# Moving the weight split and the rotary tables between engines at the start of a two-layer decoder trunk

## The chip, the cores and the metric

The kernel runs on one core of one Trainium2 chip. The metric is the device time of one execution in microseconds (us). Three executions of the kernel before gave 498.42, 498.47 and 500.37 us; their median is 498.47 us. One more execution was recorded by the hardware profiler, and every row shown below comes from that one.

A core has five engines that matter here, each with its own queue that is worked strictly in order: TensorE for matrix products (PE in the profile; its weight loads are PEld), VectorE (DVE), ScalarE (ACT), GpSimd (POOL) and SyncE (SP), which here only starts transfers (DMA).

## The reference

Two layers (`DEPTH = 2`) over 512 tokens of width 1024. A layer normalizes the stream, multiplies it with one wide matrix, splits the product into four groups of heads, mixes each in its own way, gates them, and adds the output projection to the stream:

```
h = rmsnorm(x, norm_g)
p = h @ w_in                                   # 1024 -> 3488 columns
(cq, ckv, kr, g_a, c_h, c_b, c_c, g_b, sg_u, sg_v, g_c, mq, mk, mv, g_d) = split(p)
q  = rmsnorm(cq)  @ mla_w_uq                   # latent attention, rotary part by rope(...)
kv = rmsnorm(ckv) @ mla_w_ukv
o_a = causal attention(q, k, v)
o_b = c_b * short_conv(c_c * c_h, conv_w)
o_c = spatial_gate(sg_u, sg_v, ...)
o_d = moba_attention(mq, mk, mv)               # rotary on a quarter of each head
y = concat(o_a*silu(g_a), o_b*silu(g_b), o_c*silu(g_c), o_d*silu(g_d))
x = x + y @ w_out
```

`rope(x, pos)` turns pairs of columns by the angle `pos * 500000^(-2i/32)`. So a table of 16 cosines and 16 sines for each of the 512 tokens is needed: two tiles of 128 partitions x 4 x 16.

## The kernel before, in words

**Precision.** TensorE multiplies in a shortened float format. So each operand is split in two: a high half (the value rounded to that format) and a low half (the value minus the high half), and each product is three matmuls: high x high, low weight x high, high weight x low. For a weight tile the names are `raw_` (as loaded), `whi_` and `wlo_`; for the stream they are `hTh` and `hTl`. The q projection of latent attention uses `whi_uq`, the kv projection `whi_ukv`, the next projection `raw_sq` (split into `yTh` and `yTl`, which serve as its weight tiles).

**The first stage** (`c_first`, inside `main`) computes `cq`: the first 416 columns of layer 0. It runs over the 8 slices k of 128 rows of the weight. For each k, TensorE transposes the slice of x (`xT`, four transposes), ACT rounds it to `hTh` (`x_parts`), DVE makes `hTl`, and then come 4 matmuls (one per group of 128 tokens) with `whi·hTh`, 4 with `wlo·hTh`, 4 with `whi·hTl`. The slices 6 and 7 come in another order: token group by token group, so that the first group is finished early. ACT also squares x for the normalization (`junk`, accumulated in `xsum`, in `x_stats`). The four weight tiles `c0` to `c3` are each split in two halves by `split_units`: the high half on DVE (a copy), the low half by `low_half`, on GpSimd for nearly all of them (`LOVEC = 1`).

**The rotary tables** (`rope_tables`) are worked out on DVE between that work: the angle is brought into a small range in three steps, halved, and the sine and cosine of the half are summed as polynomials, one after the other, in tiles of 128 x 64 (`rope_scratch`, results `sinT` and `cosT`).

**What sets the order.** Nothing here is ordered by hand. While the kernel is written out, a planner (`Order`, `Chain`) keeps an estimated clock for each engine (`o.clk["V"]`, `["A"]`, `["G"]`) and lets many small generators take turns; each call of `ch.dve`, `ch.act`, `ch.pool` or `ch.pe` writes one instruction and moves a clock on. Several choices are made by these clocks: which engine splits a later weight tile (line 419), which one applies the rotation (`on_dve`, line 763), and which one squares for a norm (`head_sums`, line 777). So an edit in the first 30 us changes the order, and some of the engines, of instructions much later. The instruction streams that result are fixed: on the chip an engine waits for its next instruction, however late that is.

**Loads.** `load_units` issues the weight loads on SyncE's queue in a fixed order. A tile of weights can be loaded when its `raw` buffer is free, and the queue runs only a limited number of transfers ahead: the profile shows an issue waiting for the landing of an earlier transfer.

**Later stages.** After `cq` come q and kv (`low_chain`), the big projections (`sq`, `kv`, `ga` and so on), both attentions, the mixer and the output projection (`seven`), and the same for layer 1. `rms` factors are made on GpSimd as a power (`pow_rstd`; rows `xv`, `ms`, `mq`, `mk`, `mmq` on POOL). `krt` is the shared rotary key; `t0a` are the first transposes of latent attention.

Of the kernel before, what the change touches and what calls it, by code (L numbers as in the profile page):

```python
# [33 lines left out]
AHEAD = 4  # L34
NWARM, FILL, FILLEND = 6, 0.9, 15000.0
MIXT, MIXLAG, ROWT, GT = 42000.0, 2000.0, 27000.0, 27000.0
KSPLIT, SQPOOL, LOVEC = 6, 700.0, 1
PAIRS = {}
LOPRIO = -5
ROPEB, ROPES = 400.0, 900.0  # L40
EARLY = ('sq0', 'sq1', 'sq2')
YORDER, YCUT = (2, 3, 0, 1, 4, 6, 5, 7), 6
WORDER = (1, 0, 2, 3)
# [14 lines left out]
def split_const(v, bits):  # L58

    e = math.floor(math.log2(abs(v))) + 1  # L60
    q = 2.0 ** (e - bits)
    a = round(v / q) * q
    return a, v - a
# [78 lines left out]


LAT, PELAT, SLACK, PEMARGIN = 130.0, 220.0, 300.0, 80.0


def free_size(ap):
# [56 lines left out]
def cost(n):  # L204
    return max(n / 2.4, 107.0) + 2.0
# [3 lines left out]
def hybrid_trunk(ctx: ExitStack, tc: tile.TileContext, x, positions, norm_g, w_c, w_f, w_t, w_o, mla_q_norm_g,  # L209
# [3 lines left out]
    V, A, G, PE = nc.vector, nc.scalar, nc.gpsimd, nc.tensor  # L213
# [16 lines left out]
    o = Order()  # L230
# [171 lines left out]
    def split_units(i0, i1):  # L402
        for u in order[i0:i1]:
            ch = Chain(o)
            if u.name != "c0_0":
                yield from ch.wait(u.loaded)
            u.hi, u.lo = yield from u.slots.get(ch, u.name)
            n = u.a * u.b
            for i in range(2):
                if u.name == "c0_0":  # L410
                    yield from ch.wait(u.landed[i])
                while ch.t > o.now + SLACK:
                    yield ch.t - SLACK
                while not u.wanted and max(o.clk["A"], o.clk["V"]) > o.now + WSLACK:
                    yield o.now + 100.0
                sl = slice(i * n // 2, (i + 1) * n // 2)
                c2 = Chain(o, max(o.now, ch.t))
                hi, lo, raw = u.hi[:, sl], u.lo[:, sl], u.raw[:, sl]
                if o.clk["V"] + 600.0 < o.clk["A"] or u.idx < 4:
                    yield from c2.dve_fast(V.tensor_copy, hi, raw)  # L420
                else:
                    yield from c2.act(A.activation, hi, raw, AF.Copy)
                if u.idx < 4:
                    o.set(u.high[i], c2.t)
                    o.spawn(low_half(u, i, c2, lo, raw, hi), None, LOPRIO)
                    continue
                yield from c2.dve(V.tensor_tensor, lo, raw, hi.bitcast(F32), op=ALU.subtract)
            if u.idx < 4:
                continue
            ch.t = c2.t  # L430
            u.raw_slots.put(ch)
            o.set(u.ready, ch.t)

    def low_half(u, i, ch, lo, raw, hi):
        if i == 0 or u.idx < LOVEC or o.clk["V"] + 300.0 > o.clk["G"]:
            yield from ch.pool(G.tensor_tensor, lo, raw, hi.bitcast(F32), op=ALU.subtract)
        else:
            yield from ch.dve(V.tensor_tensor, lo, raw, hi.bitcast(F32), op=ALU.subtract)
        o.set(u.half[i], ch.t)
        if u.half[1 - i].t is not None:  # L440
            ch.t = max(ch.t, u.half[1 - i].t)
            u.raw_slots.put(ch)
            o.set(u.ready, ch.t)
# [42 lines left out]
    G.tensor_copy(junk[0:NT, P:2 * P], junk[0:NT, 0:P].bitcast(I32))  # L486
    for i in range(16):
        G.memset(inv[:, i:i + 1], THETA ** (-i * 2.0 / 32))
    rope_ev = Event()

    def rope_tables():
        ch = Chain(o)
        sc = yield from t2S.get(ch, "rope_scratch")
        def carve(i):
            return sc[:, i * 64:(i + 1) * 64].rearrange("p (t i) -> p t i", t=NT)

        ang, z, cp, sp = (carve(i) for i in range(4))
        kk = [carve(4 + i) for i in range(3)]

        ch.slack = ROPES  # L500

        def on_vector():
            while max(o.clk["V"], ch.t) > o.now + ROPES:
                yield max(o.clk["V"], ch.t) - ROPES

        def dv(f, *a, **k):
            yield from on_vector()
            yield from ch.dve(getattr(V, f), *a, **k)

        def stt(out, in0, c, in1, op0, op1):  # L510
            yield from on_vector()
            yield from ch.dve(V.scalar_tensor_tensor, out, in0=in0, scalar=c, in1=in1, op0=op0, op1=op1)

        for t in range(NT):
            yield from dv("tensor_scalar", ang[:, t, :], inv, posf[:, t:t + 1], None, op0=ALU.mult)
        magic = 12582912.0
        r1, r2 = [], []
        for k, m in zip(kk, (2.0 ** 22, 2.0 ** 11, 1.0)):
            c = TWO_PI * m
            ca, cr = split_const(c, 13)  # L520
            cb, cc = split_const(cr, 13)
            yield from dv("tensor_scalar", k, ang, 1.0 / c, magic, op0=ALU.mult, op1=ALU.add)
            yield from dv("tensor_scalar", k, k, magic, None, op0=ALU.subtract)
            yield from stt(ang, k, -ca, ang, ALU.mult, ALU.add)
            r1.append((k, cb))
            r2.append((k, cc))
        for k, c in r1 + r2:
            yield from stt(ang, k, -c, ang, ALU.mult, ALU.add)
        yield from dv("tensor_scalar", ang, ang, 0.5, None, op0=ALU.mult)
        yield from dv("tensor_tensor", z, ang, ang, op=ALU.mult)  # L530
        yield from dv("tensor_scalar", sp, z, -1.0 / math.factorial(15), None, op0=ALU.mult)
        yield from dv("tensor_scalar", cp, z, 1.0 / math.factorial(16), None, op0=ALU.mult)
        for n in (14, 12, 10, 8, 6, 4, 2):
            yield from stt(cp, cp, (-1.0) ** (n // 2) / math.factorial(n), z, ALU.add, ALU.mult)
            if n > 2:
                yield from stt(sp, sp, (-1.0) ** ((n - 1) // 2) / math.factorial(n - 1), z, ALU.add, ALU.mult)
        yield from dv("tensor_scalar", cp, cp, 1.0, None, op0=ALU.add)
        yield from stt(sp, sp, 1.0, ang, ALU.add, ALU.mult)
        yield from stt(sinT, sp, 2.0, cp, ALU.mult, ALU.mult)
        yield from dv("tensor_tensor", z, sp, sp, op=ALU.mult)  # L540
        yield from dv("tensor_scalar", cosT, z, -2.0, 1.0, op0=ALU.mult, op1=ALU.add)
        t2S.put(ch)
        o.set(rope_ev, ch.t)

    def bcast(src, offset, n, name):
# [86 lines left out]
    xsum = cst.tile([P, NT, KT // 2], F32, name="xsum")  # L632
    xv = cst.tile([P, 5, NT], F32, name="xv")
    v_ev, r_ev, rh_ev = Event(), Event(), Event()
    one_box, rh_box, rh_put = [], [], shared(hS, 14)
    RV, RR, RE, RE64, REE = range(5)

    def rv(i, t):
# [53 lines left out]
    def x_row():  # L692

        ch = Chain(o)
        yield from ch.wait(r_ev)
        d = yield from t2S.get(ch, "rd")
        yield from ch.pool(G.tensor_tensor, d.rearrange("p (t c) -> p t c", t=NT),
                           ident.unsqueeze(1).to_broadcast([P, NT, P]),
                           xv[:, RR, :].unsqueeze(2).to_broadcast([P, NT, P]), op=ALU.mult)
        tp = yield from trS.get(ch, "rrow")  # L700
        yield from ch.pe(4 * cost(S), PE.matmul, tp, one_box[0][:, 0:P].bitcast(F32), d, start=True, stop=True)
        zzS.put(ch)
        t2S.put(ch)
        rh_box.append((yield from hS.get(ch, "rh")))
        yield from ch.act(A.activation, rh_box[0][:, 0:S], tp, AF.Copy, scale=0.5)
        trS.put(ch)
        o.set(rh_ev, ch.t)
# [1032 lines left out]
    def start():  # L1740
        o.clk["D"] = 1000.0
        cw = Chain(o)
# [1 line left out]
            xk[kp] = yield from v4S.get(cw, f"x{kp}_0", [P, NT, 2 * P], F32)  # L1744
        load_xk(0, 1)
        wp = yield from sS.get(cw, "warm")
        one_box.append((yield from zzS.get(cw, "ones", F32R)))
        ones = one_box[0][:, 0:P].bitcast(F32)
        V.memset(ones, 1.0)
        A.activation(xsum[:, 0, 0:1], ones[:, 0:1], AF.Square, scale=D ** -0.5)  # L1750
# [2 lines left out]
            o.fill()  # L1753
        PE.transpose(wp[:, 256:256 + NT + KT], junk[0:NT + KT, P:2 * P], ident[0:NT + KT, 0:NT + KT])
        V.tensor_copy(pg, wp[:, 256:256 + NT + KT])
        o.pe_end, o.fill_until = 3300.0, FILLEND
        o.clk["V"] = 3700.0

        def fill_end():
# [73 lines left out]
```

## Time and profile before

| what | value |
|---|---|
| median of three executions | 498.47 us |
| the profiled execution's own time | 498.7 us |
| its span, first to last instruction | 497.0 us |
| PE busy | 486.4 us (98%) |
| DVE busy | 401.6 us (81%) |
| ACT busy | 311.7 us (63%) |
| POOL busy | 158.1 us (32%) |
| data moved by DMA | 81.98 MB |

The profiled execution took 1.7 us more than its span, which lies around it. A timeline row reads: start in us, duration in us, engine, line, operation, output<-inputs, shape, count, and in brackets how long the engine had been idle and what ended that. Line 166 and line 196 are the planner's helpers through which nearly all instructions are written, so rows are told apart by their tiles. Row groups (`x8 | 8.7, 1107`) give the count, the sum in us and the mean in ns. Rows of waits give: who waited, for whom, us in total, times, longest. A row of the windows view gives the stretch, then the busy us (and number of instructions) of each engine, the granted TensorE clock (1.00 is full), the DMA share and GB/s.

### The profile page before, as it was taken

To read this page: it belongs to the slowest core of one execution; us is meant where nothing else is said; L and a number is where in the kernel's file an instruction comes from. 1 tells how busy PE (TensorE), PEld (TensorE's weight loads), DVE (VectorE), ACT (ScalarE), POOL (GpSimd) and SP (SyncE) were. 2 spreads that over 40 slices of the span, in tenths; PEclk is the share of its full clock that TensorE was granted. 3 is DMA by queue.
4 is the path that set the end of the run, shared out by engine and by line. 5 is a ranking of instruction groups with operands and counts; after the bars stand their busy time and mean duration, and the time that the engine had idled before them with its cause. 6 is when DMAs were issued, how large, how long until landed. Compare 5 with 4: busy or idle time off the path is not lost.

```text
span 497.0 us, 7795 instructions
## 1 busy us (share of the span) xinstructions
PE 486.4 (98%) x2457; PEld 412.8 (83%) x2457; DVE 401.6 (81%) x1046; ACT 311.7 (63%) x899; POOL 158.1 (32%) x276
## 2 busy tenths in 40 slices
PE   8889999999999999999999999999999999999996
PEld 8677887888888888888889988888888888888886
DVE  6979986677989878689799789577888889665982
ACT  5579754587786784346566895575757676524640
POOL 4437996544132013100042478435441010000000
PEclk9999999999999999999999999999999999999999
DMA  8635539535377126876573242557449465475652
GB/s 282 196 104 178 171 106 225 190 69 102 118 219 185 51 71 192 296 274 212 166 260 128 85 117 97 211 129 141 93 134 251 167 171 105 167 261 188 226 175 85
DMA packets 37393, 81.98 MB, mean 165 GB/s; under 512 B 7132, under 2 KB 19432, under 8 KB 37096
## 3 DMA queue, kind: packets, MB, share of 16 engines
q1 hardware_dynamic: 28880, 73.09, 43.9%
q0 software_dynamic: 8448, 8.39, 11.3%
q8 instruction: 19, 0.31, 0.3%
q14 instruction: 22, 0.18, 0.1%
q10 hardware_dynamic: 24, 0.01, 0.0%
HBM read 73.61 MB, written 24.64 MB: 198 GB/s over the span
## 4 chain that ended last, share of the span: by engine, by line
PE 83%; DMA 5%; POOL 4%; ACT 3%; DVE 2%; issue 1%; SPq 1%; POOLq 0%
PE kv L196 8%; PE oy L196 6%; PE sq L196 5%; PE ch L196 4%; PE cc L196 4%; PE gd L196 4%; PE cb L196 4%; PE gb L196 4%; PE su L196 4%; PE gc L196 4%; PE ox L196 4%; PE oz L196 4%; PE sa L196 3%; PE cq L196 3%; PE ga L196 2%; PE oa L196 2%
## 5 line engine op out<-in xcount | busy, mean ns | idle before, releaser
L166 ACT ACTIVATE pd<-pd,mnd 128x256 f32<-128x256 f32 (+3 forms) x52 | 28.0, 550 | 2.6 <-DVE mnd L166 2.5
L166 ACT ACTIVATE pa<-pa,mna 128x256 f32<-128x256 f32 (+3 forms) x45 | 24.5, 558 | 5.5 <-DVE mna L166 5.5
L166 ACT ACTIVATE pha<-pTa 128x512 fp32r<-128x512 f32 (+3 forms) x32 | 13.8, 436 | 21.1 <-PE pTa L196 21.0
L196 PE MATMUL kv<-whi_kv,hTh 128*128 128x512 f32 x64 | 26.6, 416 | 0.0
L166 POOL TENSOR_TENSOR chs<-chs,rh 128x512 f32<-128x512 f32 x6 | 9.3, 1545 | 51.7 <-ACT chs L166 37.2
L196 PE MATMUL kv<-whi_kv,hTl 128*128 128x512 f32 x64 | 25.1, 392 | 0.0
L196 PE MATMUL kv<-wlo_kv,hTh 128*128 128x512 f32 x64 | 25.0, 391 | 0.0
L341 POOL DMA_DIRECT2D t<-in_w_o_dram x16 | 18.0, 1147 | 21.5 <-DMA t<-t 13.5
L166 DVE TENSOR_TENSOR pla<-pTa,pha 128x512 fp32r<-128x512 f32 (+3 forms) x32 | 15.3, 485 | 11.7 <-ACT pha L166 11.6
L166 ACT ACTIVATE phd<-pTd 128x512 fp32r<-128x512 f32 (+3 forms) x32 | 13.8, 436 | 17.0 <-PE pTd L196 16.8
L196 PE MATMUL cq<-whi_c,hTl 128*128 128x416 f32 x64 | 20.2, 361 | 2.7 <-DVE hTl L166 2.5
L166 DVE TENSOR_TENSOR wlo_t<-raw_t,whi_t 128x512 fp32r<-128x512 f32 x32 | 21.9, 708 | 0.9 <-ACT whi_t L166 0.9
L196 PE MATMUL cq<-whi_c,hTh 128*128 128x416 f32 x64 | 20.7, 369 | 1.1 <-ACT hTh L166 1.1
L166 ACT ACTIVATE whi_t<-raw_t 128x512 fp32r<-128x512 f32 x31 | 17.7, 621 | 4.0 <-DMA raw_t<-t 4.0
L196 PE MATMUL cq<-wlo_c,hTh 128*128 128x416 f32 x64 | 20.0, 359 | 0.0
L166 DVE CUSTOM_DVE_ANT_0 pa<-sa,maskb 128x512 f32<-128x512 f32 (+3 forms) x32 | 15.1, 484 | 5.7 <-PE pTa L196 3.1
L196 PE MATMUL sq<-yTh,hTh 128*128 128x512 f32 x48 | 19.0, 395 | 0.5 <-ACT krt L166 0.5
L196 PE MATMUL sq<-yTh,hTl 128*128 128x512 f32 x48 | 18.7, 390 | 0.0
L196 PE MATMUL sq<-yTl,hTh 128*128 128x512 f32 x48 | 18.7, 390 | 0.0
L166 DVE CUSTOM_DVE_ANT_0 pd<-sd,maskb 128x256 f32<-128x256 f32 (+3 forms) x32 | 15.2, 484 | 3.4 <-PE pTd L196 3.1
L166 DVE TENSOR_TENSOR pld<-pTd,phd 128x512 fp32r<-128x512 f32 (+3 forms) x32 | 15.4, 486 | 2.6 <-ACT phd L166 2.5
L166 DVE TENSOR_TENSOR wlo_b<-raw_b,whi_b 128x512 fp32r<-128x512 f32 x24 | 15.8, 687 | 0.7 <-ACT whi_b L166 0.7
(419 smaller groups left out, 1857.7 us busy)
## 6 DMA issues: line engine op xcount, KB each, us to landing
t<-in_w_o_dram POOLq DMA_DIRECT2D x16, 512.0 KB, 7.3
raw_t<-t SPq DMA_DIRECT2D x16, 512.0 KB, 4.5
raw_b<-in_w_o_dram SPq DMA_DIRECT2D x12, 512.0 KB, 4.5
raw_sq<-in_w_t_dram SPq DMA_DIRECT2D x8, 512.0 KB, 3.7
t<-in_w_o_dram SPq DMA_DIRECT2D x8, 512.0 KB, 4.3
raw_kv<-in_w_t_dram SPq DMA_DIRECT2D x8, 512.0 KB, 3.5
t<-t SPq DMA_DIRECT2D x8, 512.0 KB, 5.5
ys<-ysc SPq DMA_DIRECT2D x14, 256.0 KB, 5.4
```

The costliest lines, as they stand in the source:

```text
L166: f(*a, **k)
L196: f(*a, **k)
L341: nc.gpsimd.dma_start(z_src(l, n, j), quad(l, b, j), accum_op=ALU.add, max_dma_last_dim=1024)
```

## The change

Four edits, all in the start of layer 0:

- `low_half` now puts every low half of the first projection's weights on DVE.
- `split_units` puts the high half of `c0` to `c3` on ACT, except the very first half tile, which stays on DVE.
- `rope_tables` runs on GpSimd. Its fused multiply-adds become two instructions each (`stt` is now a `tensor_scalar` into `tmp` and a `tensor_tensor`). The two polynomials are laid side by side (`both`, 128 x 2 x 64) and summed in common operations, with the coefficients as a small table `coef` that is filled by 15 memsets in the unused end of the tile `ones`; so that tile is taken at the start of the program (`run_now`) and given back by two users (`zz_put`).
- Planner constants: the tables may be written 1500 instead of 900 ns ahead, and the fill matmuls at the start are planned from 3700 instead of 3300.

Built, the two programs differ as follows before the first matmul with a `sq` weight. DVE loses all 40 table instructions and 7 copies, and gains the 8 subtractions that POOL loses. ACT gains 7 roundings of `whi_c` and loses one of `whi_uq`. POOL gains 15 memsets and 52 table instructions: 24 with a scalar, 15 on two tiles of 128x64 and 13 on two tiles of 128x128. SyncE's first 29 instructions are the same. Further on, the planner decides some things otherwise: the squares for the q norms of token groups 0 and 1 go from POOL and DVE to ACT, the rotation of `krt` goes from DVE to POOL, that of `Q` for groups 0 and 2 from POOL to DVE and for group 3 the other way, and `t0a` stands 32 instructions later in PE's order.

```diff
-KSPLIT, SQPOOL, LOVEC = 6, 700.0, 1
+KSPLIT, SQPOOL = 6, 700.0
...
-ROPEB, ROPES = 400.0, 900.0
+ROPEB, ROPES = 400.0, 1500.0
...
+def run_now(gen):
+
+    try:
+        next(gen)
+    except StopIteration as e:
+        return [e.value]
...
-                if o.clk["V"] + 600.0 < o.clk["A"] or u.idx < 4:
+                if o.clk["V"] + 600.0 < o.clk["A"] and u.idx > 3 or u.idx == 0 and i == 0:
                     yield from c2.dve_fast(V.tensor_copy, hi, raw)
                 else:
                     yield from c2.act(A.activation, hi, raw, AF.Copy)
...
     def low_half(u, i, ch, lo, raw, hi):
-        if i == 0 or u.idx < LOVEC or o.clk["V"] + 300.0 > o.clk["G"]:
-            yield from ch.pool(G.tensor_tensor, lo, raw, hi.bitcast(F32), op=ALU.subtract)
-        else:
-            yield from ch.dve(V.tensor_tensor, lo, raw, hi.bitcast(F32), op=ALU.subtract)
+        yield from ch.dve(V.tensor_tensor, lo, raw, hi.bitcast(F32), op=ALU.subtract)
...
+    one_box = run_now(zzS.get(Chain(o), "ones", F32R))
+    coef = one_box[0][:, 256:272].bitcast(F32).rearrange("p (f i) -> p f i", f=2)
+    zz_put = shared(zzS, 2)
+    for i in range(8):
+        G.memset(coef[:, 0, i:i + 1], (-1.0) ** (8 - i) / math.factorial(16 - 2 * i))
+        if i < 7:
+            G.memset(coef[:, 1, i:i + 1], (-1.0) ** (7 - i) / math.factorial(15 - 2 * i))
...
         def dv(f, *a, **k):
-            yield from on_vector()
-            yield from ch.dve(getattr(V, f), *a, **k)
+            yield from ready()
+            yield from ch.pool(getattr(G, f), *a, **k)

         def stt(out, in0, c, in1, op0, op1):
-            yield from on_vector()
-            yield from ch.dve(V.scalar_tensor_tensor, out, in0=in0, scalar=c, in1=in1, op0=op0, op1=op1)
+            yield from dv("tensor_scalar", tmp, in0, c, None, op0=op0)
+            yield from dv("tensor_tensor", out, tmp, in1, op=op1)
...
-        yield from dv("tensor_scalar", sp, z, -1.0 / math.factorial(15), None, op0=ALU.mult)
-        yield from dv("tensor_scalar", cp, z, 1.0 / math.factorial(16), None, op0=ALU.mult)
-        for n in (14, 12, 10, 8, 6, 4, 2):
-            yield from stt(cp, cp, (-1.0) ** (n // 2) / math.factorial(n), z, ALU.add, ALU.mult)
-            if n > 2:
-                yield from stt(sp, sp, (-1.0) ** ((n - 1) // 2) / math.factorial(n - 1), z, ALU.add, ALU.mult)
+
+        yield from dv("tensor_tensor", both, coef[:, :, 0:1].to_broadcast([P, 2, 64]), zz2, op=ALU.mult)
+        for i in range(1, 8):
+            n = 2 if i < 7 else 1
+            yield from dv("tensor_tensor", both[:, 0:n, :], both[:, 0:n, :],
+                          coef[:, 0:n, i:i + 1].to_broadcast([P, n, 64]), op=ALU.add)
+            yield from dv("tensor_tensor", both[:, 0:n, :], both[:, 0:n, :], zz2[:, 0:n, :], op=ALU.mult)
...
-        o.pe_end, o.fill_until = 3300.0, FILLEND
+        o.pe_end, o.fill_until = 3700.0, FILLEND
```

More of the change, by code (lines that the diff above doesn't have):

```diff
@@ L498, in rope_tables, with ready @@
         kk = [carve(4 + i) for i in range(3)]
+        tmp = carve(7)
+        both = sc[:, 2 * 64:4 * 64].rearrange("p (f x) -> p f x", f=2)
+        zz2 = sc[:, 64:2 * 64].unsqueeze(1).to_broadcast([P, 2, 64])
         ch.slack = ROPES
-        def on_vector():
-            while max(o.clk["V"], ch.t) > o.now + ROPES:
-                yield max(o.clk["V"], ch.t) - ROPES
+        def ready():
+            while max(o.clk["G"], ch.t) > o.now + ROPES:
+                yield max(o.clk["G"], ch.t) - ROPES
         def dv(f, *a, **k):
-            yield from on_vector()
-            yield from ch.dve(getattr(V, f), *a, **k)
+            yield from ready()
+            yield from ch.pool(getattr(G, f), *a, **k)
         def stt(out, in0, c, in1, op0, op1):
-            yield from on_vector()
-            yield from ch.dve(V.scalar_tensor_tensor, out, in0=in0, scalar=c, in1=in1, op0=op0, op1=op1)
+            yield from dv("tensor_scalar", tmp, in0, c, None, op0=op0)
+            yield from dv("tensor_tensor", out, tmp, in1, op=op1)
         for t in range(NT):
@@ L542, in rope_tables @@
         t2S.put(ch)
+        zz_put(ch)
         o.set(rope_ev, ch.t)
@@ L634, in hybrid_trunk @@
     v_ev, r_ev, rh_ev = Event(), Event(), Event()
-    one_box, rh_box, rh_put = [], [], shared(hS, 14)
+    rh_box, rh_put = [], shared(hS, 14)
     RV, RR, RE, RE64, REE = range(5)
@@ L701, in x_row @@
         yield from ch.pe(4 * cost(S), PE.matmul, tp, one_box[0][:, 0:P].bitcast(F32), d, start=True, stop=True)
-        zzS.put(ch)
+        zz_put(ch)
         t2S.put(ch)
@@ L1746, in start @@
         wp = yield from sS.get(cw, "warm")
-        one_box.append((yield from zzS.get(cw, "ones", F32R)))
         ones = one_box[0][:, 0:P].bitcast(F32)
```

## The prediction

> **What bounds the kernel now.** I read the page's busy times first, then PE's waits, then the timeline, then the chain of waits.
>
> ```profile
> span 497.0 us, 7795 instructions
> PE 486.4 (98%) x2457; PEld 412.8 (83%) x2457; DVE 401.6 (81%) x1046; ACT 311.7 (63%) x899; POOL 158.1 (32%) x276
> ```
>
> TensorE does nothing for 10.6 of 497.0 us. The waits of PE over the whole execution say where, besides the start and the end of the kernel:
>
> ```profile
> PE cq L196 <- DVE hTl L166: 2.5, 3, 1.0
> PE cq L196 <- ACT hTh L166: 1.1, 2, 0.8
> PE hT L196 <- DVE hTl L166: 0.7, 1, 0.7
> PE sq L196 <- ACT krt L166: 0.5, 1, 0.5
> PE t0a L196 <- DVE Q L166: 0.4, 1, 0.4
> ```
>
> The first projection (`cq`) loses 3.6 us, everything behind it 1.6 us. So nearly all that this change can win lies in the first stage, and it is at most 3.6 us there. The timeline shows why DVE is late with `hTl`:
>
> ```profile
> 5.84 1.08 POOL L166 TENSOR_TENSOR wlo_c<-raw_c,whi_c 128x416 fp32r<-128x416 f32 x1 [2.77 <-DVE whi_c L166]
> 5.89 1.10 DVE L166 SCALAR_TENSOR_TENSOR rope_scratch<-rope_scratch 128x64 f32<-128x64 f32 x1
> ...
> 13.73 0.74 DVE L166 SCALAR_TENSOR_TENSOR hTl<-xT,pg,hTh 128x512 fp32r<-128x512 f32 x1
> 14.53 1.03 PE L196 MATMUL cq<-whi_c,hTl 128*128 128x416 f32 x4 [0.61 <-DVE hTl L166]
> ```
>
> A small table instruction on DVE lasts as long as the subtraction that runs on POOL beside it (1.10 beside 1.08), `hTl` stands behind it in DVE's queue, and PE waits. The change takes both of that pair away from each other. But the chain of waits of the same stretch is another one:
>
> ```profile
> 5.60 8.95 DMA raw_c<-in_w_c_dram
> 14.56 5.09 DMA lg_b<-in_sg_ln_g_dram
> 19.73 5.85 DMA raw_sq<-in_w_t_dram
> 25.61 0.63 ACT yTh L166
> 26.24 0.40 ACT junk L166 x2
> 26.64 0.58 ACT hTh L166
> ```
>
> Three transfers, each issued when the one before has landed, end at 25.58 us with the first weights of the next projection. ACT's queue has its rounding (`yTh`) ahead of a square and of `hTh` of slice 6, so slice 6 cannot start earlier:
>
> ```profile
> 27.27 0.46 PE L196 MATMUL cq<-whi_c,hTh 128*128 128x416 f32 x1 [0.75 <-ACT hTh L166]
> ```
>
> **The change part by part.** The sums are made against the profiled execution's own 498.7 us (span 497.0 and 1.7 around it), 0.23 above the median of 498.47.
>
> *Low halves, POOL to DVE.*
>
> ```profile
> L166 DVE TENSOR_TENSOR wlo_uq<-raw_uq,whi_uq 128x384 fp32r<-128x384 f32 x2 | 1.1, 548 | 0.0
> L166 DVE CAST whi_c<-raw_c 128x416 fp32r<-128x416 f32 x8 | 2.7, 370 | 0.0
> L166 DVE SCALAR_TENSOR_TENSOR rope_scratch<-rope_scratch 128x64 f32<-128x64 f32 x23 | 9.6, 446 | 0.3
> L166 ACT ACTIVATE whi_uq<-raw_uq 128x384 fp32r<-128x384 f32 x2 | 0.9, 510 | 0.0
> ```
>
> Scaled by 416/384 one subtraction takes 0.59 us on DVE. That is the lower end; the upper is 0.59 plus a whole POOL instruction waited out (1.08), 1.67. I take 0.8, since the POOL instructions now beside it are short (below): 8 x 0.8 = 6.4 us on DVE. Off DVE go 7 copies (2.6 us) and the table instructions, 9.6 us for one group of them alone. DVE is relieved by at least 5.8 us in a stage where its lateness costs 2.5.
>
> [...]
>
> *High halves, DVE to ACT.* 7 x 0.55 (0.510 scaled) = 3.9 us more for ACT, less 0.5 for the half of `whi_uq` that leaves. ACT has room in these 27 us:
>
> ```profile
> ACT hTh L166 <- PE xT L196: 7.4, 6, 2.3
> ACT yTh L166 <- DMA raw_sq<-in_w_t_dram: 2.9, 1, 2.9
> ```
>
> It waits 7.4 us for PE's transposes and 2.9 for the transfer. Cost nothing: were that cover gone, up to 3.4 us.
>
> *Tables, DVE to POOL.*
>
> ```profile
> L166 POOL TENSOR_SCALAR dq_b<-dq_b 128x64 f32<-128x64 f32 x1 | 0.4, 384 | 0.0
> L166 POOL TENSOR_TENSOR rbq<-Q,sinT 128x64 f32<-128x64 f32 x6 | 2.0, 333 | 0.4 <-ACT junk L166 0.3
> L166 POOL TENSOR_TENSOR squares<-K 128x256 f32<-128x256 f32 x1 | 0.6, 612 | 0.0
> L166 POOL TENSOR_TENSOR Q<-Q,cosT 128x64 f32<-128x64 f32 x6 | 3.9, 657 | 0.1
> 30.25 1.42 POOL L166 TENSOR_TENSOR xv<-xv,nhalf 128x4 f32<-128x4 f32 x1 [8.84 <-DVE xv L166]
> ```
>
> 24 x 0.384 + 15 x 0.333 + 13 x 0.43 (a third of the way from 0.333 to 0.612) = 19.8 us; the nearest slow row, beside a busy DVE, has 0.657, which for all 52 gives 34.2. POOL's order puts the power for the x norm (`xv`) behind 40 of the 52: begun at about 5 us, as now on DVE, they end at about 20, and at 40 x 0.657 + 5 = 31.3 at worst, when that power starts now at 30.25. So 0, at worst 1.1 on POOL. Twelve table instructions follow it, between the other powers: 4.6 to 7.9 us.
>
> *What PE gains.* Undisturbed slices show its pace:
>
> ```profile
> 9.11 0.93 PE L196 MATMUL cq<-whi_c,hTh 128*128 128x416 f32 x4
> 9.87 0.60 PE L196 MATMUL xT<-ident,x 128*128 128x128 f32 x4
> 10.22 1.00 PE L196 MATMUL cq<-wlo_c,hTh 128*128 128x416 f32 x4
> 11.82 0.91 PE L196 MATMUL cq<-whi_c,hTh 128*128 128x416 f32 x4
> ```
>
> One slice takes 11.82 - 9.11 = 2.71 us. The row at 11.82 begins slice 2; slices 2 to 5 at that pace and the one additional transpose among them (10.22 - 9.87 = 0.35) end at 11.82 + 4 x 2.71 + 0.35 = 23.0 us. Now they end at 26.5 (27.27 less the wait of 0.75). And then PE waits. In the changed program ACT still has `yTh`, a square, `hTh` of slice 6, `yTh`, a square, `hTh` of slice 7, in that order, and SyncE's transfers up to there are the same. Slice 6 starts at 27.27 as now. Gain: 0. What was four waits becomes one of about 4.3 us.
>
> *Behind it.* The order of the last 24 `cq` matmuls is unchanged. What is added there is ACT's: the squares of q for two token groups,
>
> ```profile
> L166 ACT ACTIVATE junk<-Q x8: 270/274/288, 46.2 to 52.8; 128x96 f32<-128x96 f32 x8
> L166 ACT ACTIVATION_READ_ACCUMULATOR junk<-Q x8: 188/190/196, 46.4 to 53.0; 128x1 f32 x8
> 40.00:45.00 5.00, 4.91 (x24) 4.09 (x24) 4.74 (x15) 4.81 (x21) 2.90 (x3) 1.00 0.53 180
> 61.68 0.39 ACT L166 ACTIVATE mq<-sq 128x256 f32<-128x256 f32 x1 [2.43 <-DVE bst L166]
> ```
>
> 8 x (0.274 + 0.190) = 3.7 us of busy time at most, in a stretch in which ACT (fourth figure, 4.81 of 5.00) is full. ACT also empties the PSUM tiles that q and kv need, so PE can lose 0 to 3.7 us; ACT's first real pause (2.43 us) is only at 61 us. I take 0.4: nearer to 0, because in the new order PE has `sq` work to do between q and kv. Sum: 0 + 0.4, so 498.9 against the median.
>
> **The rivals.**
>
> *The clock drops in the long wait (slower).*
>
> ```profile
> 492.97 0.28 PE L196 MATMUL ot<-whi_b,yTl 128*128 128x256 f32 x1
> ...
> 496.20:496.30 0.10, 0.00 (x0) 0.00 (x0) 0.00 (x0) 0.00 (x0) 0.00 (x0) 0.50 0.00 0
> ```
>
> After the last matmul (ended 493.25) the granted clock is halved at 496.2, about 3 us later. A wait of 4.3 us is longer; today's waits, 1.0 at most, end before that. Against it: DVE's new contention may make PE slower before the wait and so shorten it. The price is unknown. The lower end is 0; the upper is all 24 remaining matmuls at double their 0.19 (0.76 for four), 4.6 us more. I take 3 us at half clock, as long as the clock took to fall, so 1.5 us lost, of which the 0.5 us wait for `krt` takes up a third: 1.0, and with the 0.4 the time is 499.9.
>
> [...]
>
> *The end of the stage is not held by the transfer (faster).* If `raw_sq` landed by about 21.5 us, PE would go on at 23.0 and win up to the 3.6 us of its waits: 494.9. For it speaks that DVE is truly relieved; against it that the three transfers wait for each other and for no engine. It decides from a landing 1 us earlier.
>
> *POOL comes late (slower).*
>
> ```profile
> 60.00:80.00 20.00, 20.00 (x95) 16.63 (x94) 18.33 (x55) 9.11 (x30) 18.82 (x30) 1.00 0.60 131
> ```
>
> POOL (the fifth engine, 18.82 of 20.00) is full from 60 to 80 us. The last 12 table instructions and the rotation of `krt` (6 x 0.657 = 3.9) push 8 to 12 us in ahead of that; the two squarings (0.9 each, scaled from the 0.612) and, net, twelve rotation instructions that leave POOL (six at 0.333 to 0.657, six half as wide) take back 5 to 8. A net 3 to 4 us would reach `t0a`, were it not 32 instructions (7 us) later in PE's order. If it does: 501.5 to 503.
>
> **How the numbers follow.** Held by the transfer at full clock, 498.9: 0.42. The clock drop, 499.9 (to 503 at the upper end): 0.32. POOL or ACT late beyond their cover, 501.5 to 503: 0.13. The transfer does not hold: 0.08. The last 0.05 is for the planner's other order in later stages, either way; PE's 1.6 us of waits there leave little to win. A difference of 0.5% (2.5 us) is about what this measurement can tell from no change. Faster: 0.08 + 0.02 = 0.10. Slower: 0.13 + 0.06 of the clock drop's upper part + 0.02 = 0.21. Same: the rest, 0.69. The range, 496.8 to 502.0, leaves out most of the faster case and the top of the late ones.
>
> **What would show it.** Right: PE reaches the end of slice 5 near 23 us and waits some 4 us for ACT `hTh`; `yTh` still waits for `raw_sq` at about 25.6, longer than 2.9 us; the waits of `cq` for `hTl` shrink below 1 us; the first `sq` matmul is near 34 us. The clock rival: a granted clock of 0.5 between 25 and 31 us. Wrong: a first `sq` matmul before 32 us, or new waits of PE above 2 us between 40 and 100 us.

## The result and the profile after

The changed kernel takes 501.05 us (median of 20 executions, 498.45 to 502.85) against 498.56 for the kernel before (498.15 to 500.41): ratio 1.0043, 95% interval 1.0029 to 1.0056. It is slower by 2.5 us. The profiled execution took 501.79 us.

The busy times of the changed kernel's page:

```profile
span 500.1 us, 7817 instructions
PE 489.4 (98%) x2455; PEld 416.3 (83%) x2455; DVE 395.9 (79%) x1014; ACT 314.9 (63%) x918; POOL 162.5 (32%) x327
```

The span is 3.1 us longer, and TensorE is idle as long as before (500.1 - 489.4 = 10.7 us, before 10.6). What grew is its busy time, by 3.0 us, for the same work. So in sum the loss stands in the pace of the matmuls. The waits of PE add up as before, but they changed their place and shape (those from 0.3 us on, without the start):

```profile
PE cq L204 <- ACT hTh L174: 2.6, 1, 2.6
PE kv L204 <- ACT mix L174: 2.3, 1, 2.3
PE hT L204 <- DVE hTl L174: 0.7, 1, 0.7
PE ga L204 <- DVE vn L174: 0.3, 1, 0.3
```

`cq` no longer waits for `hTl`. Its short waits have become one of 2.6 us for `hTh` of slice 6, and a second long one (2.3 us, `kv` for the mixer's `mix`) is new. The timeline of PE at the first (start, duration, engine, line, operation, and in brackets the idle time before):

```profile
22.63 1.00 PE L204 MATMUL cq<-whi_c,hTl 128*128 128x416 f32 x4
26.26 0.46 PE L204 MATMUL cq<-whi_c,hTh 128*128 128x416 f32 x1 [2.62 <-ACT hTh L174]
26.55 0.35 PE L204 MATMUL cq<-wlo_c,hTh 128*128 128x416 f32 x1
27.04 0.52 PE L204 MATMUL cq<-whi_c,hTl 128*128 128x416 f32 x1
27.36 0.55 PE L204 MATMUL cq<-whi_c,hTh 128*128 128x416 f32 x1
27.71 0.55 PE L204 MATMUL cq<-wlo_c,hTh 128*128 128x416 f32 x1
...
33.52 0.40 PE L204 MATMUL sq<-yTh,hTh 128*128 128x512 f32 x1
```

Slice 5 ends near 23.6 us. Slice 6 begins 2.62 us later, and from 27.36 on the matmuls start 0.35 us apart instead of 0.19. The windows of the same stretch (stretch, its length, busy time of PE, PEld, DVE, ACT and POOL, granted clock, DMA share, GB/s) give the reason:

```profile
24.00:25.00 1.00, 0.00 (x0) 0.00 (x0) 0.00 (x0) 0.40 (x1) 0.00 (x0) 1.00 0.69 279
27.00:28.00 1.00, 0.96 (x3) 0.92 (x4) 0.85 (x2) 1.00 (x4) 0.00 (x0) 0.64 0.00 0
28.00:29.00 1.00, 1.00 (x4) 0.95 (x4) 1.00 (x3) 1.00 (x4) 0.00 (x0) 0.50 0.61 82
30.00:31.00 1.00, 1.00 (x5) 0.97 (x5) 1.00 (x4) 0.63 (x4) 0.00 (x0) 0.65 0.50 201
```

The granted clock is still full in the pause (24 to 25 us) and falls to half at 27.3 us, 1.0 us after PE has gone back to work. It stays there until 30.7, for 3.4 us (both times worked out from the means of the windows). At a granted clock of 0.50 such a stretch costs at most half its length, by my estimate 1.7 us. The pause itself is the one that the chain of waits shows, and here its end is the transfer of `raw_sq`:

```profile
19.79 4.79 DMA raw_sq<-in_w_t_dram
24.60 0.63 ACT yTh L174
25.23 0.40 ACT junk L174 x2
25.63 0.58 ACT hTh L174
```

The second pause, as ACT's and PE's timelines show it:

```profile
82.62 0.63 ACT L174 ACTIVATE whi_su<-raw_su 128x512 fp32r<-128x512 f32 x1 [5.13 <-DMA raw_su<-in_w_f_dram]
83.16 0.46 ACT L174 ACTIVATE mix<-mp,sgb 128x256 f32<-128x256 f32 x1
...
84.55 0.50 PE L204 MATMUL kv<-whi_kv,hTh 128*128 128x512 f32 x1 [2.25 <-ACT mix L174]
...
85.37 0.63 PE L204 MATMUL kv<-whi_kv,hTh 128*128 128x512 f32 x1
85.80 0.63 PE L204 MATMUL kv<-wlo_kv,hTh 128*128 128x512 f32 x1
```

In ACT's queue the rounding of the mixer's weights (`whi_su`) stands ahead of all four evictions of the mixer's PSUM tiles (`mix`). It waits 5.13 us for its load, and PE waits behind it for a PSUM tile. 0.8 us after PE has resumed its pace falls to half again (0.43 us between starts from 85.37 on, instead of 0.23); the windows have the granted clock at 0.50 from 85.3 to 88.7 us. In the kernel before, three of the four evictions stood ahead of `whi_su`, and PE had no wait here above 0.4 us:

```profile
80.10 0.48 ACT L166 ACTIVATE mix<-mp,sgb 128x256 f32<-128x256 f32 x1 [0.54 <-PE mp L196]
82.88 0.63 ACT L166 ACTIVATE whi_su<-raw_su 128x512 fp32r<-128x512 f32 x1 [2.31 <-DMA raw_su<-in_w_f_dram]
83.42 0.46 ACT L166 ACTIVATE mix<-mp,sgb 128x256 f32<-128x256 f32 x1
```

By the same estimate two stretches of 3.4 us at half clock cost 3.4 us, which is the 3.0 us by which PE's busy time grew, to within half a microsecond. At the first `sq` matmul the changed kernel is still 0.5 us ahead of the kernel before (33.52 against 34.01), and at the end it is 3.1 us behind, so the net loss arises behind the first projection.

### The profile page after: what moved, and what is told of

Its sections match the earlier page's. It is cut to its first block, busy times and chain, and to the rows that moved or that the text cites. A ratio compares the mean times of both kernels' runs of the same rounds, so it can differ in the third digit from the quotient of the medians.

```text
span 500.1 us, 7817 instructions
## 1 busy us (share of the span) xinstructions
PE 489.4 (98%) x2455; PEld 416.3 (83%) x2455; DVE 395.9 (79%) x1014; ACT 314.9 (63%) x918; POOL 162.5 (32%) x327
## 4 chain that ended last, share of the span: by engine, by line
PE 82%; DVE 7%; DMA 4%; ACT 3%; SPq 2%; issue 1%; POOL 0%; ACTq 0%
PE kv L204 9%; PE oy L204 6%; PE sq L204 5%; PE gb L204 4%; PE cb L204 4%; PE gd L204 4%; PE su L204 4%; PE oz L204 4%; PE ox L204 4%; PE cq L204 4%; PE cc L204 4%; PE gc L204 4%; PE ch L204 3%; PE sa L204 3%; PE ga L204 2%; PE sd L204 2%
## 5 line engine op out<-in xcount | busy, mean ns | idle before, releaser
L174 ACT ACTIVATE pha<-pTa 128x512 fp32r<-128x512 f32 (+3 forms) x32 | 13.8, 435 | 23.9 <-PE pTa L204 23.9
L174 ACT ACTIVATE pd<-pd,mnd 128x256 f32<-128x256 f32 (+3 forms) x49 | 26.2, 545 | 2.9 <-DVE mnd L174 2.8
L204 PE MATMUL kv<-whi_kv,hTl 128*128 128x512 f32 x64 | 25.6, 400 | 0.0
L204 PE MATMUL cq<-whi_c,hTh 128*128 128x416 f32 x64 | 21.8, 387 | 2.6 <-ACT hTh L174 2.6
L174 DVE CUSTOM_DVE_ANT_0 pd<-sd,maskb 128x384 f32<-128x384 f32 (+3 forms) x32 | 15.2, 483 | 2.4 <-PE pTd L204 1.7
```

Of the source, the lines that this page charges most:

```text
L174: f(*a, **k)
L204: f(*a, **k)
```

## The experiments

All times are medians, with the ratio to runs of the kernel before on the same chip, which took 498.37 to 498.79 us there.

**The two halves of the change.** e8 makes only the weights' part: the two edits below in the kernel before. e7 makes only the tables' part: the changed kernel with these two edits undone (it keeps the changed planner constants).

```diff
-                if o.clk["V"] + 600.0 < o.clk["A"] or u.idx < 4:
+                if o.clk["V"] + 600.0 < o.clk["A"] and u.idx > 3 or u.idx == 0 and i == 0:
...
-        if i == 0 or u.idx < LOVEC or o.clk["V"] + 300.0 > o.clk["G"]:
-            yield from ch.pool(G.tensor_tensor, lo, raw, hi.bitcast(F32), op=ALU.subtract)
-        else:
-            yield from ch.dve(V.tensor_tensor, lo, raw, hi.bitcast(F32), op=ALU.subtract)
+        yield from ch.dve(V.tensor_tensor, lo, raw, hi.bitcast(F32), op=ALU.subtract)
```

> Only the weights change (low halves on DVE, high halves on ACT); the rotary tables stay on DVE. DVE then has the 9.6 us of table instructions and 8 subtractions of about 0.6. If DVE's load is what makes hTl late, the waits of cq for hTl stay (1 to 3 us in all), slice 6 starts near 26 to 27 us as held by the transfer, the pause stays in short pieces, and the clock stays at 1.00: 498 to 499.5. If the overlap with GpSimd alone was the cause, the hTl waits vanish and one long wait with half clock appears, as in the changed kernel: 500 to 501.

> Only the rotary tables go to GpSimd; the weights are split as before (high halves on DVE, low halves on GpSimd or DVE). If the pairing of a table instruction on DVE with a subtraction on GpSimd was what made hTl late, the waits of cq for hTl shrink below 1 us, slice 5 ends early, and one wait of 2 us or more for ACT hTh appears with half clock behind it, as in the changed kernel. If GpSimd instead becomes late with the subtractions that now stand between table instructions, PE waits for POOL wlo_c in several short waits, the clock stays at 1.00, and the time is 498 to 500. I give the second 0.6.

e8: 498.87 us, ratio 1.0009 (0.9997 to 1.0021). e7: 499.52 us, ratio 1.0022 (1.0013 to 1.0031). In both, `cq`'s waits for `hTl` are gone (0.2 us left in e8, none listed in e7). For e7 that, with one long wait and half clock behind it, was the side that I held less likely. e8 fits neither of its two sides whole: the waits went as the second said, the time lies in the range of the first, and the profiled execution has no half clock (four of the ten executions have a mean clock of 0.993 to 0.997). DVE carries the tables and the subtractions in e8, one instruction more than before, and is not late. The groups of instructions on DVE in e8 from 4 to 28 us (busy us, mean ns of one):

```profile
L166 DVE SCALAR_TENSOR_TENSOR rope_scratch<-rope_scratch 128x64 f32<-128x64 f32 x23 | 4.7, 220 | 0.2
L166 DVE TENSOR_TENSOR wlo_c<-raw_c,whi_c 128x416 fp32r<-128x416 f32 x8 | 4.7, 586 | 0.2 <-ACT whi_c L166 0.2
```

The 23 table instructions take 4.7 us in place of 9.6 (220 ns each in place of 446), and nothing runs on GpSimd beside them (POOL is busy for 0.00 us from 5 to 30 us): the subtractions cost less than the tables save by running alone. So it was the overlap, in which these instructions took twice as long on average, that made `hTl` late, and not their number. Moving either of the two off its engine is enough.

The two runs then meet the transfer in different ways. PE's timelines, first two rows e8, then e7:

```profile
6.95 1.76 PE L196 MATMUL cq<-whi_c,hTh 128*128 128x416 f32 x4
26.14 0.45 PE L196 MATMUL cq<-whi_c,hTh 128*128 128x416 f32 x1 [0.57 <-ACT hTh L166]
```

```profile
26.47 0.72 PE L204 MATMUL cq<-whi_c,hTh 128*128 128x416 f32 x1 [3.25 <-ACT hTh L174]
```

In the profiled execution of e8 the first matmuls ran at about half pace (1.76 us for four in place of 1.03; full pace only from 10.7 us on), PE came to slice 6 late by that, and only 0.57 us of waiting was left. (That slow start isn't why `hTl` is in time: e12 below starts at full pace, four matmuls in 1.02 us, and has no wait for `hTl` either.) In e7 PE waited 3.25 us, and the windows of e7 show what follows:

```profile
24.00:25.00 1.00, 0.00 (x0) 0.00 (x0) 0.04 (x1) 0.70 (x2) 0.54 (x2) 1.00 0.77 315
26.00:31.00 5.00, 4.53 (x13) 4.05 (x14) 4.42 (x10) 3.03 (x9) 1.75 (x4) 0.50 0.29 105
31.00:32.00 1.00, 1.00 (x5) 0.95 (x4) 0.84 (x2) 0.76 (x5) 0.86 (x3) 0.50 0.50 164
```

Half clock from 25.6 to 32.4 us, two stretches of 3.4 us in a row. Slice 6 starts between 26.1 and 27.3 us in the kernel before, the changed one, e7 and e8, whoever carries which part.

**Taking away the first drop of the clock (e1).** Nine matmuls into a PSUM tile that nobody reads are put between slices 5 and 6 (18 records in the profile); they change nothing that is computed, and the order of all other work stays.

```diff
             o.fill_until = 0.0
-            sS.put(Chain(o))
             return
...
+            for _ in range(9):
+                o.fill()
+            sS.put(Chain(o))
             for t, k in ((0, 6), (1, 6), (0, 7), (1, 7), (2, 6), (2, 7), (3, 6), (3, 7)):
```

> The changed kernel with nine fill matmuls in PE's queue between slice 5 and slice 6 of the first projection (about 2.4 us of work that nothing uses), every other instruction where it was. Theory clock: the wait for slice 6 no longer lets the granted clock fall, the 24 cq matmuls behind it run at full clock, and the first sq matmul comes about 1.6 us earlier; the second long wait of PE (2.3 us, at 82 us) stays, and may even grow by the time won, because the load that ends it does not move: 499.4 to 500.9, median about 500.0 where the changed kernel has 501.05. Theory order: the loss comes from the planner's other order of the later stages alone, and the slow clock of the first stage was hidden by waits: no change, 500.9 to 501.2.

Measured: 499.14 us, ratio 1.0020 (1.0004 to 1.0035), granted clock 1.00 in all windows up to 90 us.

```profile
23.19 2.17 PE L1769 MATMUL warm<-ones 128*128 128x128 f32 x18
26.66 0.46 PE L204 MATMUL cq<-whi_c,hTh 128*128 128x416 f32 x1 [1.30 <-ACT hTh L174]
...
32.84 0.50 PE L204 MATMUL sq<-yTh,hTh 128*128 128x512 f32 x1
...
83.47 0.51 PE L204 MATMUL kv<-whi_kv,hTh 128*128 128x512 f32 x1 [1.71 <-ACT mix L174]
```

Slice 6 starts no earlier than in the changed kernel (26.66 against 26.26), but after a pause of 1.30 instead of 2.62 us, and no half clock follows. The time is 1.9 us lower, a little below the expected range. It isn't the price of one stretch: the first `sq` matmul comes 0.7 us earlier, where 1.6 was expected, and the second drop is gone too: the wait for `mix`, expected to stay at 2.3 us or grow, is 1.71 us, and no half clock follows it. e1 thus takes both stretches away in its profiled execution (ten of its twelve have a mean clock of 0.999 or 1.00), and its time is that of the changed kernel's own two executions without a drop (498.45 and 499.43).

**Taking away the second long wait (e3, control e6).** The split of `su0` waits until the mixer's evictions are in ACT's queue. e6 does the same in the kernel before.

```diff
             if u.name != "c0_0":
                 yield from ch.wait(u.loaded)
+            if u.name == "su0_0":
+                yield from ch.wait(layers[0].mix_ev)
```

> The changed kernel with the rounding of the su0 weights held back until the mixer's four evictions (mix) are written, so that ACT does not wait for the su0 load ahead of them. Nothing before 75 us changes. Theory wait: PE's wait of 2.3 us for mix goes, and with it the second fall of the clock (about 1.7 us): 497 to 498.5. Rival: PE then waits for the su0 weights themselves, which are wanted soon after; the wait only moves: 500.5 to 501.5.

> The kernel before with the load of su0 held in the same way. There three of the four mixer evictions stand ahead of that load already, and PE waits 0.4 us at most nearby. If the hold helped the changed kernel because it took a wait of PE away, it has nothing to take here: 498.6 (497.9 to 499.5), clock 1.00. If the hold is worth something by itself, through the order that the planner then finds, the time falls by 1 us or more, to 497.5 or less.

e3: 497.57 us, ratio 0.9980 (0.9966 to 0.9994), 3.5 us below the changed kernel. PE has no wait for `mix` any more, the 2.6 us wait for `hTh` is unchanged, and the first drop is still there. e6: 499.81 us, ratio 1.0030 (1.0018 to 1.0042), above the range that I had given for no effect; its wait of `t0a` for DVE `Q` grew from 0.4 to 1.1 us. Since the planner orders several hundred later instructions anew in both, the control matters: the hold is worth nothing by itself there, it costs 1.4 us. That what it brings to the changed kernel comes from the wait that it takes away is the likely reading. The new order of the later work isn't separated from it.

**Both together (e5).**

> The changed kernel with both edits at once: nine matmuls that compute nothing between slices 5 and 6 of the first projection, and the load of su0 held until the mixer's four evictions are in ACT's queue. If the loss is the two long waits and the half clock behind each, the parts add: about 497.6 less 1.9, so 495.7 (495.0 to 496.6), granted clock 1.00 throughout, no wait of PE for ACT mix, the wait for ACT hTh at 1.3 us or so. If holding su0 helped only because the planner's order came out well, or the clock's loss is covered by later waits, the two do not add: 497.2 to 498.5.

Measured: 496.81 us, ratio 0.9967 (0.9956 to 0.9977). The two gains add in part: 496.8 where 495.7 was expected, though not 497.2 or more. They could not add whole, as e1's 1.9 us hold the second drop, which e3 takes away as well. The profiled execution of e5 shows why the fill is a poor remedy:

```profile
23.82 2.17 PE L1771 MATMUL warm<-ones 128*128 128x128 f32 x18
27.85 0.46 PE L204 MATMUL cq<-whi_c,hTh 128*128 128x416 f32 x1 [1.86 <-ACT hTh L174]
...
29.13 0.55 PE L204 MATMUL cq<-wlo_c,hTh 128*128 128x416 f32 x1
29.47 0.55 PE L204 MATMUL cq<-whi_c,hTl 128*128 128x416 f32 x1
```

`raw_sq` landed 1.6 us later there (26.17 us), the rest of the pause was 1.86 us, and the clock fell at 29.1 us after all. That execution took 498.58 us, the longest of its 11.

**Making slice 6 independent of the transfer through ACT's order (e2, and e4 in the kernel before).** The split of `sq0` and `sq1` waits until `hTh` of slice 7 is in the queue.

```diff
+            if u.name in ("sq0_0", "sq1_0"):
+                yield from ch.wait(xhi[KT - 1])
```

> The changed kernel with the rounding of the first two sq weight tiles held back until hTh of slice 7 is written, so that ACT's queue has nothing that waits for raw_sq ahead of slices 6 and 7 (the planner reorders from there on). Theory transfer: it was that queue position alone which pinned the stage; slice 6 starts near 23.5 us instead of 26.3 to 27.3, there is no long wait and no fall of the clock, and the first sq matmul comes at about 29 us instead of 33.5: 494 to 498. Rival: something else holds the stage (the x transposes, DVE, the first sq weights themselves), the first sq matmul stays after 32 us, and the time is 499 to 502.

> The kernel before with the same holding back of the first two sq weight tiles. Theory transfer: in the kernel before PE comes to slice 6 at 26.5 us and waits only 0.75 us there, so little is to be had: 497.3 to 498.6, at most 1.2 us. If the queue position costs the kernel before as much as the changed one (2.6 us and more), it falls below 496.5, and the relief of DVE would not be needed for that gain.

e2: 502.37 us, ratio 1.0074 (1.0060 to 1.0088). e4: 505.20 us, ratio 1.0133 (1.0120 to 1.0146). Both lie above all that was expected of them. PE works without a pause from 22 to 26 us in e2 and the first `sq` matmul comes at 31.29, so the transfer no longer holds slice 6, and the waits come back behind it:

```profile
PE sq L204 <- DVE vn L174: 3.1, 1, 3.1
PE sq L204 <- DVE wlo_sq L174: 2.4, 2, 1.3
PE sq L204 <- ACT krt L174: 1.2, 1, 1.2
```

The weights of `sq` are now late themselves. These two runs don't settle the matter, as the edit also moves the later work of every engine.

**Moving the transfer itself (e9, control e10).** The first two transfers of `raw_sq` go ahead of the small parameter transfers on SyncE's queue (there are thirteen, not the fifteen of the expectation). No instruction changes its place on any compute engine.

```diff
-        LOAD_HOOKS["ukv_0"] = (lambda: load_params(L0),)
+        LOAD_HOOKS["sq1_0"] = (lambda: load_params(L0),)
```

> The changed kernel with the first two transfers of raw_sq moved on SyncE's queue ahead of the fifteen small parameter transfers; no compute engine's order changes. If the landing of raw_sq is what holds slice 6, ACT's wait for it goes, slice 6 starts within 0.8 us of the end of slice 5 (23.3 to 24.4 us instead of 26.26), no half clock follows, and the whole 2.6 us and the 1.7 us of half clock are won as far as the end: 496.2 to 498.0, with the wait for ACT mix still there (1.7 to 3 us). If the next thing in the chain (the parameters, which now land later, krt, the low halves of sq) is only a little less late, the wait moves behind slice 7, as it did when ACT's order was changed: PE waits of 2 us or more in sq between 28 and 36 us, and 499 to 501.

> The same move in the kernel before. There PE reaches the end of slice 5 only at 26.5 us because of its three waits for hTl, so an earlier landing has only the 0.75 us wait to take: 497.6 to 498.6, and the three waits for hTl stay at 2.5 us. If instead the transfer was the true bound of this stage in the kernel before too, with the hTl waits only filling the time up to it, the time falls by 2 us or more: 496.5 or less.

e9: 495.00 us, ratio 0.9930 (0.9918 to 0.9943), 6.1 us below the changed kernel and better than expected. e10: 498.76 us, ratio 1.0003 (0.9994 to 1.0011), just above its range for no gain. The timeline of PE and the longest wait in e9:

```profile
24.03 1.00 PE L204 MATMUL cq<-whi_c,hTl 128*128 128x416 f32 x4
24.86 0.35 PE L204 MATMUL cq<-whi_c,hTh 128*128 128x416 f32 x1
25.06 0.35 PE L204 MATMUL cq<-wlo_c,hTh 128*128 128x416 f32 x1
```

```profile
PE kv L204 <- ACT mix L174: 1.7, 1, 1.7
```

Slice 6 follows slice 5 without a pause at full pace. The wait for `mix` is still there but at 1.7 us, and no half clock follows it (the profiled execution's mean clock is 0.999). That is where the expectation was too high: I had left the second drop in. The parts account for it: 2.6 us of wait, 1.7 of half clock, and 0.6 + 1.7 at the second place make 6.6 us against 6.1 measured. Only 12 of the changed kernel's 20 executions have both stretches, so the sum is an upper figure. In e10 nothing was won, not even the 0.75 us wait for `hTh`, because the waits of `cq` for `hTl` took it up (2.9 us in four instead of 2.5 in three). In the kernel before the transfer is covered by DVE's lateness; in the changed one it is the bound.

**The sum of both remedies (e11), and the weights alone with the transfer moved (e12).** e11 is the changed kernel with the edits of e9 and e3, e12 is e8 with the edit of e9.

> The changed kernel with both waits taken at their causes: raw_sq ahead of the parameters, and the load of su0 held behind the mixer's evictions. If the two long waits are all that stood between the change and its gain, the time is that of the run with su0 held alone (497.6) less 2.6 and less 1.7 of half clock: 493.3 to 495.0, clock 1.00, no wait of PE above 1 us before 100 us. If the gain of the first stage is given back behind it, 496.3 to 497.6.

> The weights part alone (tables stay on DVE) with raw_sq moved ahead of the parameters, again without any other change of order. In the run with the weights alone PE was free of hTl waits and reached the end of slice 5 at about 25.5 us because its first 26 matmuls ran at half the pace; a wait of 0.6 us for the transfer was left. If overlap of table instructions with GpSimd's subtractions is all that the change had to remove, and the engine of the tables does not matter, this comes near the changed kernel with the same move (495.0): 495.0 to 497.3, the spread being the slow start. If the tables' 8 us on DVE still cost something once the transfer is gone, waits of PE for DVE (hTl, ct, krt, vn) of 2 us or more in all remain before 40 us, and the time is 497.5 to 499.

e11: 492.33 us, ratio 0.9872 (0.9858 to 0.9886), below its range (493.3 to 495.0). e12: 493.89 us, ratio 0.9903 (0.9886 to 0.9919), also below. Both beat both kernels, e11 by 6.0 us against the kernel before. Its waits of PE:

```profile
PE cq L204 <- ACT hTh L174: 1.1, 2, 0.7
PE hT L204 <- DVE hTl L174: 0.7, 1, 0.7
```

Medians in us, each row with the parameters first and with `raw_sq` first:

| | parameters first | `raw_sq` first |
|---|---|---|
| kernel before | 498.4 to 498.8 | 498.76 |
| tables alone moved (e7) | 499.52 | not run |
| weights alone moved (e8, e12) | 498.87 | 493.89 |
| whole change | 501.05 | 495.00 |
| whole change, `su0` held | 497.57 | 492.33 |

In the first column nothing is won by relieving DVE alone, and in the second 3.8 to 4.9 us. The edit of the transfer is worth 0 in the kernel before and 5 to 6 us in the others. The whole change is slower than the weights alone in both columns (by 2.2 and 1.1 us), and its order of ACT's queue brings the wait for `mix`; with that wait taken away too it is 1.6 us faster than e12. Whether e12 has something left to win from the order of `su0` was not tried.

## Why the prediction was right or wrong

The forecast of 498.9 us named the right mechanism, no gain because the transfer holds slice 6, and missed by 2.2 us, inside its range of 496.8 to 502.0. That the time lies in the range is not owed to the sum: the sum has 0.4 us behind the first projection where the profiled executions differ by 3.6, and the range was wide enough because of the rivals. The difference of 0.5% that was to be the least this measurement can tell was too cautious: the interval is about 0.13% to either side, so the 0.43% measured is clear of it. By its own steps:

- *What bounds the kernel now.* Right that the first projection is where something can be won. "At most 3.6 us there" was too low: in e12 the first `sq` matmul starts at 28.80 us, in the kernel before at 34.01. In the windows of these two stretches the same 130 matmuls are busy for 22.33 us in place of 23.77, which a list of waits doesn't show. In the kernel before, the four matmuls behind the wait of 0.61 us took 1.03 us, undisturbed ones 0.91 to 0.93; so I read the difference as overlap that PE lost at each short wait.

```profile
6.29:34.01 27.72, 23.77 (x130) 20.71 (x130) 25.49 (x67) 17.75 (x60) 11.25 (x11) 1.00 0.67 215
```

```profile
6.22:28.80 22.58, 22.33 (x130) 21.21 (x131) 20.84 (x65) 19.69 (x66) 1.43 (x2) 1.00 0.79 261
```

- *Low halves, 8 x 0.8 = 6.4 us on DVE.* A little too high:

```profile
L174 DVE TENSOR_TENSOR wlo_c<-raw_c,whi_c 128x416 fp32r<-128x416 f32 x8 | 4.8, 624 | 2.5 <-ACT whi_c L174 2.5
```

0.624 us each beside GpSimd's table instructions, 0.586 beside an idle GpSimd in e8. The table sums of 128 x 64 on GpSimd vary more, between 0.32 and 0.56 us, and the three longest (0.53 to 0.56) each run beside a subtraction on DVE. `hTl` took 0.750 us beside the table instructions, as long as beside an idle GpSimd in e8 (0.750; before 0.743), so they cost it nothing.
- *High halves on ACT, cost 0.* Right: e8 has all of that and no wait of PE from it above 0.57 us.
- *Tables on POOL, the first 40 ended by about 20 us.* The durations were right (16.3 us for 40 instructions, 0.41 each, against 0.38 taken), but I left out the gaps of about 0.09 us between them: the last ends at 23.9. The power for `xv` still waited 7.1 us for DVE, so the cost was 0 as predicted.
- *What PE gains: slice 5 ends at 23.0, slice 6 starts at 27.27 as now, gain 0.* Slice 5 ended at 23.6; half of the difference was there when slice 2 began, at 12.12 instead of 11.82. `raw_sq` landed at 24.58 instead of 25.58, though the queue's order had not changed, so slice 6 started at 26.26. The one long wait is 2.6 us instead of 4.3. The gain until the first `sq` matmul is 0.5 us, and e9 shows that the transfer holds it.
- *Behind it, 0.4 us for ACT's squares between 40 and 53 us.* Here the step failed. PE was fully busy from 40 to 60 us, and the squares cost nothing. What ACT did cost stands 30 us later and is of another kind: in the new order a rounding that waits for a load stands ahead of four evictions. I had looked at how full ACT is, and not at what waits for a transfer in its queue ahead of work that PE needs. It cost 2.3 us of wait and up to 1.7 of half clock, 3.5 in all as e3 measured it.
- *The clock rival.* I gave "held by the transfer at full clock" 0.42 and the drop 0.32; it was the drop. Of the changed kernel's 20 executions 12 had a mean granted clock of 0.992 or 0.993 (median 501.7 us), 6 of 0.996 or 0.997 (500.4), and 2 of 0.999 or 1.0 (498.45 and 499.43). One stretch of 3.4 us at half clock lowers the mean by 3.4 x 0.5 / 500 = 0.0034, so these are two, one and none. The two executions without any lie around the forecast, in part by chance, as the sum held neither the wait for `mix` nor the 0.5 us gained before. The price of one stretch was well sized: 1.5 predicted, at most 1.7 by its length, and 1.3 to 1.5 from one of these groups to the next. Its condition was not: I had taken the 3 us of the kernel's tail as the pause that it needs, and it came after 2.6 and 2.25 and, in e5, 1.86 us. Setting the `krt` wait of 0.5 us against it was right in kind: `sq` has no such wait in the changed kernel.
- *The transfer does not hold (rival, 494.9 us).* It did hold. Made untrue by e9, the time came to 495.00, as near as that by chance, since a wait of 1.7 us for `mix` is in it that the rival did not have. The remark that it decides from a landing 1 us earlier was not borne out: the transfer landed 1 us earlier, slice 6 started 1 us earlier, and it was still held.
- *POOL comes late (rival).* Not seen: no wait of PE for POOL, and `t0a` has none that is listed.
- *What would show it.* Met: slice 5 near 23 us, no wait of `cq` for `hTl` above 1 us, `yTh` waiting longer than 2.9 us for `raw_sq` (3.8), the first `sq` matmul near 34 (33.52), and the sign of the clock rival between 25 and 31 us. Not met in size: the wait for `hTh` (2.6 instead of some 4 us) and the landing of `raw_sq` (24.58 instead of about 25.6). Met as well was the sign for being wrong, a new wait of PE above 2 us between 40 and 100 us.

## What to carry to other kernels

Before an engine is relieved, follow the chain of waits to what ends second: here a transfer that could not be seen in the waits of the engine that was late, and one moved line on the DMA queue decided between 0 and 5 us. Several short waits of TensorE that became one long one cost more here than they had, since the clock halved behind it (3.6 us of waits of `cq` in the kernel before; one of 2.6 us and by estimate up to 1.7 us of half clock in the changed one); remove the cause of the pause (e9, 495.00 us) rather than fill it (e1, 499.14). Here no pause of 1.71 us or less was followed by half clock in a profiled execution, and every one of 1.86 us or more was. In an engine's queue in order, look for instructions that wait for a load ahead of evictions that TensorE needs (here ACT waited 5.13 us for `raw_su`, and PE 2.25 us behind it).

## What the runs showed of the hardware

- In the fourteen profiled executions the granted clock halved after every pause of PE from 1.86 us on (1.86 in e5, 2.25 and 2.62 in the changed kernel, 2.60 in e3, 3.1 in e2, 3.25 in e7, 4.6 in e4), and after none of 1.71 us or less (1.71 and 1.30 in e1, 1.67 in e9). In the changed kernel, e3, e5 and e7 the windows show when: it fell between 0.9 us before (e7) and 1.3 us after (e5) PE had resumed, and stayed at 0.50 for 3.4 us each time, twice that in e7. In e2 and e4 the mean from 60 to 80 us is 0.91, by estimate 3.4 to 3.8 us at half. Whether it falls differs between executions of one kernel: the mean clocks of the changed kernel's 20 lie between 0.992 and 1.0. No run shows what decides it.
- A table instruction of 128 x 64 on DVE took 446 ns on average beside GpSimd's subtractions and 220 ns without them (e8). The subtraction takes GpSimd 1.1 us in either case (1107 ns in the kernel before, 1132 ns in e7, where no table instruction runs on DVE).
- The pace at the start differed between profiled executions: full from 4.9 us on in the kernel before, from 7.3 in the changed one, from 10.7 in e8. The clock column reads 1.00 there in all three; only the durations of the matmuls tell (four transposes `xT` took 1.11 us in the changed kernel and 1.06 in e8 before that, and 0.60 after it).
- The transfer of `raw_sq`, issued at 19.7 to 21.0 us with the same work ahead of it, landed at 25.58 (before), 24.58 (changed) and 26.17 us (e5). What makes the difference was not tried.
